# Filter spectra summed in PSUM, and adaLN products placed beside other projections

## The chip, the cores and the metric

One core of one Trainium2 chip runs the whole program. The number that counts is the device time of one execution in microseconds, as the median of several runs.

## The reference, cut to what matters

Two layers run over 1024 latent tokens and 256 context tokens. In each, a mixer (attention, a long convolution called Hyena, and an mLSTM) is followed by a SwiGLU network. Each layer scales and shifts its inputs by 48 groups of 128 numbers made from a conditioning vector (adaLN); the latent tokens use one vector, the context tokens another.

```python
s_lat = jax.nn.silu(c)
s_ctx = jax.nn.silu(c_ctx)
for l in range(DEPTH):
    mod = (s_lat @ w_mod[l] + b_mod[l])[:, None, :]
    mod_c = s_ctx @ w_mod[l] + b_mod[l]
    sh1, sc1, g1, sh2, sc2, g2 = jnp.split(mod, 6, axis=-1)
    ...
    h = modulate(x, norm1_w[l], sh1, sc1)
    hc = modulate(ctx, norm1_w[l], sh1c, sc1c)
    y, yc = token_mixer(h, hc, ...)
    x = x + g1 * y
    x = x + g2 * swiglu(modulate(x, norm2_w[l], sh2, sc2), ...)
```

Inside the mixer the Hyena part needs the spectrum of a filter that a small network makes, for both orders `o`, over the latent length and, in layer 0 only, over the context length:

```python
filt = (z @ w3) * jnp.exp(-t * jnp.abs(decay))
circ = jnp.concatenate([fwd, zeros, jnp.flip(bwd[:L - 1], axis=0)], axis=0)
filt_fft = jnp.fft.rfft(circ, axis=0)
```

## The kernel before, in words

Everything stays in fp32. Most matrix products are made as three products of split halves (a high and a low part), the three lines L168, L169 and L170 in `mm3`; the kernel calls the splits `w` (weights), `hh` and `hl` (tokens). The instructions are written in Python generators; `weave` interleaves several of them by their counts (the second number of each stream, a third number being a head start), a scheduler then fixes one order for each engine, and each engine works through its own order. All weights come by DMAs that SP (SyncE) issues in its order; a tile pool with `bufs` buffers makes a load wait until the buffer's last reader is done, and what stands behind it on SP waits too.

The stages of a layer's first half are written in `project`:

- The key projections (`self.first`) are woven with the first filter taps. In layer 0 this follows the start, where `first_mod` makes adaLN groups 0 to 15 for layer 0 with matmuls.
- The **V/Q stage**: value and query projections (`project_v`, `project_q`), woven with the remaining filter taps. `filter_taps` makes two matmuls, ACT exponentials, a DVE product `ex` (L912), and the sums `eo` (L920 on DVE or POOL) that are stored to memory for each of 8 (latent, tag L) or 2 (context, tag C) residues.
- The **hyena stage**: `hyena_inputs` makes nine blocks of 128 output channels (48 products on 512 columns each and, in layer 0, 24 on 256 columns), convolves them on DVE (L459, L460), and transposes them. Woven with it is `filter_spectra`. In layer 0 alone `modulation` for groups 16 to 47 is woven in as well.

`modulation` makes one group `f` at a time for the conditioning vectors `v`: SP loads 512 KB of weights (`mraw`, L250); for layer 0 DVE multiplies them by the broadcast conditioning row `silb` and adds up each row (the `junk` operation, L263) for the latent vector; POOL multiplies in place for the other vector (L254), ACT adds that up (L271), and POOL adds the bias (L272). The pool `mr` has two `mraw` buffers there.

`filter_spectra` reads the stored taps again (`er`). For each parity `par` and order `o` it makes 14 fp32 matmuls with matrices `mf` (or 2 for the short length), each alone in a PSUM bank out of two pairs (`f0`,`f1` and `t`,`o`). ACT copies the first of a pair to `fsb` (L967), and DVE adds or subtracts the second (one line, L948, for this and for the butterflies that follow, whose names show which is which: those with `fsb` are the sums of the pairs).

In layer 0's second half, the down projection (`down`, weights `raw<-in_wdn`, loaded at L156, activations `raw<-act` at L1415) is woven with `next_mod`, which makes all of layer 1's adaLN groups with POOL and ACT alone: 48 groups for the latent vector and 16 for the context vector, three `mraw` buffers; and with layer 1's `filter_mlp` (its first matmul is L868).

## Time and profile before

| | us |
|---|---|
| median of 3 runs | 3497.43 |
| lowest and highest of them | 3488.84, 3499.35 |
| the profiled execution's own time | 3502.94 |
| span in that profile, first to last instruction | 3501.2 |
| TensorE (PE) busy | 3245.5, 93% |
| VectorE (DVE) busy | 2143.6, 61% |
| ScalarE (ACT) busy | 1383.2, 40% |
| GpSimd (POOL) busy | 1298.2, 37% |

The busy times are over the whole program; a stage can be limited by another engine than the program is. The profiled execution took 1.7 us more than its span.

### The profile page before, as it was taken

To read this page: it belongs to the slowest core of one execution; us is meant where nothing else is said; L and a number is where in the kernel's file an instruction comes from. 1 tells how busy PE (TensorE), PEld (TensorE's weight loads), DVE (VectorE), ACT (ScalarE), POOL (GpSimd) and SP (SyncE) were. 2 spreads that over 40 slices of the span, in tenths; PEclk is the share of its full clock that TensorE was granted. 3 is DMA by queue.
4 is the path that set the end of the run, shared out by engine and by line. 5 is a ranking of instruction groups with operands and counts; after the bars stand their busy time and mean duration, and the time that the engine had idled before them with its cause. 6 is when DMAs were issued, how large, how long until landed. Compare 5 with 4: busy or idle time off the path is not lost. (4 is left out here: it accounts for less than half of the span.)

```text
span 3501.2 us, 49138 instructions
## 1 busy us (share of the span) xinstructions
PE 3245.5 (93%) x17486; PEld 2764.1 (79%) x17486; DVE 2143.6 (61%) x3893; ACT 1383.2 (40%) x3049; POOL 1298.2 (37%) x1192
## 2 busy tenths in 40 slices
PE   7988999888979999998989999999888899999998
PEld 3966798878868888886867897898777578887787
DVE  8669657897494444344565756556995854444443
ACT  5444456433453322223441543355343533333210
POOL 2345323574143333334880220133662443443000
PEclk8999999898989999998999999999899999999999
DMA  6666546432711222126662364445325322223532
GB/s 232 198 198 204 164 129 185 127 92 70 209 61 52 73 72 67 63 68 237 224 223 85 119 207 152 142 122 177 98 78 162 98 73 75 82 76 100 163 97 72
DMA packets 336932, 448.75 MB, mean 128 GB/s; under 512 B 46576, under 2 KB 248996, under 8 KB 334639
## 3 DMA queue, kind: packets, MB, share of 16 engines
q1 hardware_dynamic: 336312, 445.27, 40.2%
q8 instruction: 138, 2.26, 0.3%
q14 instruction: 107, 0.88, 0.1%
q10 hardware_dynamic: 375, 0.34, 0.0%
HBM read 329.34 MB, written 116.16 MB: 127 GB/s over the span
## 5 line engine op out<-in xcount | busy, mean ns | idle before, releaser
L136 ACT ACTIVATE w<-raw 128x512 fp32r<-128x512 f32 (+3 forms) x286 | 221.0, 800 | 479.6 <-PE f L169 133.3
L168 PE MATMUL f<-b,w 128*128 128x512 f32 (+1 forms) x912 | 342.5, 386 | 44.8 <-ACT b L136 37.4
L141 DVE TENSOR_TENSOR w<-raw,w 128x512 fp32r<-128x512 f32 (+3 forms) x266 | 278.6, 1063 | 151.6 <-ACT w L136 139.6
L141 DVE TENSOR_TENSOR w<-S,w 128x512 fp32r<-128x512 f32 x168 | 145.7, 888 | 353.8 <-ACT w L136 332.9
L169 PE MATMUL f<-b,w 128*128 128x512 f32 (+1 forms) x912 | 338.6, 372 | 2.6 <-DVE b L141 2.4
L170 PE MATMUL f<-b,w 128*128 128x512 f32 (+1 forms) x912 | 336.9, 370 | 0.0
L168 PE MATMUL mm<-w,hh 128*128 128x256 f32 (+2 forms) x928 | 280.1, 302 | 9.7 <-ACT hh L326 5.1
L254 POOL TENSOR_TENSOR mraw<-mraw,silb 128x1024 f32<-128x1024 f32 x96 | 248.3, 2593 | 106.1 <-DVE mod L263 67.7
L170 PE MATMUL mm<-w,hl 128*128 128x256 f32 (+2 forms) x928 | 276.6, 300 | 5.3 <-DVE hl L327 5.3
L169 PE MATMUL mm<-w,hh 128*128 128x256 f32 (+2 forms) x928 | 278.6, 301 | 0.0
L1427 DVE SCALAR_TENSOR_TENSOR x<-f,mod,x 128x512 f32<-128x512 f32 (+1 forms) x256 | 166.6, 663 | 168.7 <-PE f L170 159.9
L168 PEld LDWEIGHTS f<-b,w 128*128 128x128 f32 x912 | 179.4, 199 | 84.4 <-ACT b L136 41.8
L169 PEld LDWEIGHTS f<-b,w 128*128 128x128 f32 x912 | 177.2, 194 | 35.9 <-DVE b L141 5.1
L170 PEld LDWEIGHTS f<-b,w 128*128 128x128 f32 x912 | 176.8, 194 | 30.0
L136 ACT ACTIVATE w<-S 128x512 fp32r<-128x512 f32 x168 | 101.1, 626 | 227.2 <-POOL S L1232 208.3
L168 PEld LDWEIGHTS mm<-w,hh 128*128 128x128 f32 x928 | 178.2, 192 | 14.4 <-ACT hh L326 7.1
L170 PEld LDWEIGHTS mm<-w,hl 128*128 128x128 f32 x928 | 176.9, 191 | 7.3 <-DVE hl L327 6.8
L169 PEld LDWEIGHTS mm<-w,hh 128*128 128x128 f32 x928 | 178.1, 192 | 0.8 <-DVE w L141 0.3
L271 ACT ACTIVATE mraw<-mraw 128x1024 f32<-128x1024 f32 x96 | 101.6, 1058 | 147.6 <-POOL mraw L254 147.3
L1294 PE MATMUL a<-hb,w 128*128 128x512 f32 x352 | 141.4, 402 | 7.9 <-DVE hb L141 7.8
L1294 PE MATMUL b<-hb,w 128*128 128x512 f32 x352 | 140.7, 400 | 8.1 <-DVE hb L141 7.9
L168 PE MATMUL mm<-hh,w 128*128 128x512 f32 (+1 forms) x360 | 143.8, 399 | 1.6 <-ACT hu L453 1.6
(685 smaller groups left out, 9255.5 us busy)
## 6 DMA issues: line engine op xcount, KB each, us to landing
mraw<-in_wmodT SPq DMA_DIRECT2D x96, 512.0 KB
raw<-in_wgu SPq DMA_DIRECT2D x88, 512.0 KB
act<-g SPq DMA_DIRECT2D x88, 256.0 KB
raw<-in_wdn SPq DMA_DIRECT2D x44, 512.0 KB
raw<-act SPq DMA_DIRECT2D x42, 512.0 KB
raw<-in_wout SPq DMA_DIRECT2D x32, 512.0 KB
q<-qd SPq DMA_DIRECT2D x144, 96.0 KB
eoL<-eo SPq DMA_DIRECT2D x64, 192.0 KB
```

The lines of the kernel that those rows point to most:

```text
L136: ins = nc.scalar.activation(out=hi, in_=src, func=AF.Copy)
L141: (eng or nc.vector).tensor_tensor(out=lo, in0=src, in1=hi.bitcast(F32), op=ALU.subtract)
L168: nc.tensor.matmul(out=ps, lhsT=ah, rhs=bh, start=(i == 0), stop=False, skip_group_check=on)
L169: nc.tensor.matmul(out=ps, lhsT=ah, rhs=bl, start=False, stop=False, skip_group_check=on)
L170: nc.tensor.matmul(out=ps, lhsT=al, rhs=bh, start=False, stop=(i % part == part - 1 or i == n - 1), skip_group_check=on)
L254: nc.gpsimd.tensor_tensor(out=raw, in0=raw, in1=sil[v], op=ALU.mult)
L271: self.nc.scalar.activation(out=raw, in_=raw, func=AF.Copy, accum_out=o)
L1294: nc.tensor.matmul(out=ps, lhsT=ah[:, ks], rhs=bl, start=False, stop=False, skip_group_check=not start)
L1427: nc.vector.scalar_tensor_tensor(out=x, in0=ps[:, :n], scalar=d["mod"][:, 40 + m, v:v + 1], in1=x, op0=ALU.mult, op1=ALU.add)
```

## The change

**Spectra.** The sum or difference of each pair is now made by two matmuls that add up in one PSUM bank, the second with `mf` or, for a difference, with its negative `mg` (new, loaded in pool "fb" at the start of the hyena stage). That is 16 matmuls for each `par` and `o` in place of 14 (4 in place of 2 for the short length). Of the eight sums five are copied by ACT (before, seven copies), the others are read from PSUM by DVE. Eight DVE sums fall away for each `par` and `o` (two for the short length). The `er` loads get four buffers.

**adaLN.** `silu_row` no longer loads the plain vector and applies Silu: the start stores the Silu rows to memory (`silr`, two DMAs on ACT's queue, each with 1024 separate 4-byte pieces) and the rows are read from there. In both layers `modulation` of groups 16 to 47 is created ahead of the filter taps' pool; the first ME = 12 groups are woven into the V/Q stage and the other 20 into the hyena stage. For layer 1 (latent vector alone, thus POOL and ACT without DVE) these 32 groups are taken out of layer 0's down stage, where 32 of 64 items remain.

```diff
@@ constants
+ME = 12, 12
@@ silu_row
         t = self.t(sp, [P, DM], F32, "silb")
-        self.nc.sync.dma_start(out=t, in_=self.A["crow"][v].partition_broadcast(P))
-        self.nc.scalar.activation(out=t, in_=t, func=AF.Silu)
+        self.nc.sync.dma_start(out=t, in_=self.silr[v].partition_broadcast(P))
         return t
@@ dft_mats
-            M[n] = self.t(hp, [P, R // 2 if n[0] == "n" else R, 2, P], F32, "m" + n)
+            M[n] = self.t(hp, [P, R // 2 if n[0] in "ng" else R, 2, P], F32, "m" + n)
@@ filter_spectra
-        pairs = [(0, 4), (2, 6), (1, 7), (3, 5)] if R == 8 else [(0, 1)]
-        turn = False
+        half = R // 2
+        neg = M["g" + tag]
+        mats = M["f" + tag]
+
+        sums = [("p0", 0, half, 0, 1), ("m0", 0, half, 0, -1)]
+        if R == 8:
+            sums = [("y1", 1, 7, 1, -1), ("x1", 1, 7, 0, 1), ("y3", 3, 5, 1, -1), ("x3", 3, 5, 0, 1)] + sums + [("y2", 2, 6, 1, -1), ("x2", 2, 6, 0, 1)]
+        banks = itertools.cycle(x for y in SB for x in y)
...
-                for pair in pairs:
-                    eo = {}
-                    for r in pair:
-                        eo[r] = new("er", 3)
-                        nc.sync.dma_start(out=eo[r], in_=EO[par][o][:, r, :])
-                    ra, rb = pair
-                    for tri in range(2):
-
-                        comp = par if tri == 0 else 1 - par
-                        if tri == 1 and ra == 0:
-                            continue
-                        turn = not turn
-                        pa, pb = (self.ps(x) for x in SB[turn])
-                        for r, pp in ((ra, pa), (rb, pb)):
-                            nc.tensor.matmul(out=pp[:, :HY], lhsT=mats[:, r, comp, :], rhs=eo[r], start=True, stop=True)
-                        sb = new("fsb", 2)
-                        nc.scalar.activation(out=sb, in_=pa[:, :HY], func=AF.Copy)
-                        if tri == 0:
-                            acc["p", ra] = tt(new(f"accp{ra}"), sb, pb[:, :HY], ALU.add, nc.vector)
-                            if ra == 0:
-                                acc["m", ra] = tt(new("accm"), sb, pb[:, :HY], ALU.subtract, nc.vector)
-                        else:
-                            acc["y", ra] = tt(new(f"accy{ra}"), sb, pb[:, :HY], ALU.subtract, nc.vector)
-                    yield
+                acc, eo = {}, {}
+                for name, ra, rb, tri, sign in sums:
+                    if ra not in eo:
+                        for r in (ra, rb):
+                            eo[r] = new("er", 4)
+                            nc.sync.dma_start(out=eo[r], in_=EO[par][o][:, r, :])
+                    comp = 1 - par if tri else par
+                    ps = self.ps(next(banks))[:, :HY]
+                    mb = mats[:, rb, comp, :] if sign > 0 else neg[:, rb - half, comp, :]
+                    nc.tensor.matmul(out=ps, lhsT=mats[:, ra, comp, :], rhs=eo[ra], start=True, stop=False)
+                    nc.tensor.matmul(out=ps, lhsT=mb, rhs=eo[rb], start=False, stop=True)
+                    if name in ("x3", "y3", "x2"):
+                        acc[name] = ps
+                    else:
+                        acc[name] = new(name)
+                        nc.scalar.activation(out=acc[name], in_=ps, func=AF.Copy)
+                    if name == "y3":
+                        s13 = tt(new("s13"), acc["y1"], ps, ALU.add)
+                        R2 = tt(acc["y1"], acc["y1"], ps, ALU.subtract)
+                    elif name == "x3":
+                        P0 = tt(new("P0"), acc["x1"], ps, ALU.add)
+                        D_ = tt(acc["x1"], acc["x1"], ps, ALU.subtract)
+                    if sign < 0:
+                        yield
...
@@ first_mod
         nc.scalar.activation(out=sil, in_=sil, func=AF.Silu)
+        self.silr = self.dram([2, DM], "silr")
+        for v in range(2):
+            nc.scalar.dma_start(out=self.silr[v].rearrange("(k p) -> p k", p=P), in_=sil[:, :, v])
@@ project
+            sp, silp, mr = (mst.enter_context(self.pool(x, bufs=b, side="right")) for x, b in (("md", 1), ("sl", 2), ("mr", 2)))
+            sil = [self.silu_row(silp, v) for v in range(2 - last)]
+            junk = (DM, lambda: self.t(sp, [P, DM], BF16, "junk"))
+            mods = self.modulation(l, [(f, range(2 - last)) for f in range(16, 48)], mr, "mraw", junk, sil, range(16, 48))
             with self.pool("fa", side="right") as fa:
                 taps = chain(*(self.filter_taps(l, R, t, fa) for t, R in tags))
                 weave((self.first, (10, 4)[l]), (self.take(taps, TK[l]), TK[l]))
                 self.lnexp(False)
                 D["G"] = self.gates(l, D)
-                weave((chain(self.project_v(l, D, pj), self.project_q(l, D, pj)), 10 + nt), (taps, TV[l]))
-            mods = []
-            if l == 0:
...
-                self.lnexp()
...
+                weave((chain(self.project_v(l, D, pj), self.project_q(l, D, pj)), 10 + nt), (taps, TV[l]), (self.take(mods, ME[l]), ME[l]))
             with self.pool("fb") as fb, self.pool("hi", side="right") as hi:
-                weave((self.hyena_inputs(l, D, hi), 18 if last else 27), *((g, 32) for g in mods),
-                      (chain(*(self.filter_spectra(l, R, t, M["f" + t], fb) for t, R in tags)), 36))
-            if l == 0:
-                self.mod_done(0, 4)
+                self.dft_mats(fb, ["g" + t for t, _ in tags], M)
+                weave((self.hyena_inputs(l, D, hi), 18 if last else 27), (mods, 32 - ME[l]),
+                      (chain(*(self.filter_spectra(l, R, t, M, fb) for t, R in tags)), 20 if last else 24))
+            if last:
+                nc.vector.memset(self.L[1]["mod"][:, 16:48, 1], 0.0)
+            self.mod_done(l, 4)
@@ second
-                    m = chain(*(self.next_mod(v, n, sp, mr) for v, n in ((0, 48), (1, 16))))
-                    weave((f, 28), (m, 70, 14), (self.filter_mlp(l + 1, fs), *FW))
-                nc.vector.memset(self.L[1]["mod"][:, 16:48, 1], 0.0)
+                    m = chain(*(self.next_mod(v, n, sp, mr) for v, n in ((0, 16), (1, 16))))
+                    weave((f, 28), (m, 34, 6), (self.filter_mlp(l + 1, fs), *FW))
                 self.mod_done(1, 1)
-                self.mod_done(1, 4)
@@ tables
-        A["mn" + tag] = np.ascontiguousarray(-mf[:, R // 2:].astype(f))
+        A["mg" + tag] = A["mn" + tag] = np.ascontiguousarray(-mf[:, R // 2:].astype(f))
```

The order of instructions, at three places. Numbers at the end of a name count the tiles.

SP in layer 0's down stage, where the loads of adaLN weights (`mraw`) meet those of the down projection (`raw<-in_wdn`, and `raw<-act`). Before:

```order
L250 DMA mraw_17131<-in_wmodT 128x1024
L250 DMA mraw_17157<-in_wmodT 128x1024
L250 DMA mraw_17218<-in_wmodT 128x1024
L156 DMA raw_16461<-in_wdn 128x1024
L250 DMA mraw_17223<-in_wmodT 128x1024
L156 DMA raw_16467<-in_wdn 128x1024
L250 DMA mraw_17296<-in_wmodT 128x1024
L250 DMA mraw_17301<-in_wmodT 128x1024
L156 DMA raw_16473<-in_wdn 128x1024
L250 DMA mraw_17306<-in_wmodT 128x1024
L156 DMA raw_16479<-in_wdn 128x1024
L250 DMA mraw_17367<-in_wmodT 128x1024
```

And now, at the same activations and the same first weights of the down projection:

```order
L252 DMA mraw_17448<-in_wmodT 128x1024
L252 DMA mraw_17453<-in_wmodT 128x1024
L252 DMA mraw_17458<-in_wmodT 128x1024
L1414 DMA raw_16268<-act_2047_9396 128x2x512
L252 DMA mraw_17463<-in_wmodT 128x1024
L1414 DMA raw_16274<-act_2048_9397 128x2x512
L158 DMA raw_16336<-in_wdn 128x1024
L158 DMA raw_16342<-in_wdn 128x1024
L158 DMA raw_16348<-in_wdn 128x1024
L158 DMA raw_16354<-in_wdn 128x1024
```

Before, eight loads of adaLN weights stood ahead of this group's first down weight and more between the weights; now the last loads of adaLN weights of the stage stand ahead of this group's two activations, and its four down weights follow each other.

DVE at the end of layer 0's V/Q stage (`ex` and `eo` are the last filter taps, `w` are weight splits, `junk` with `mod` is one adaLN group). Before:

```order
L912 TENSOR_TENSOR ex_1885<-f_385_1887,ex_1885 128x384
L912 TENSOR_TENSOR ex_1885<-f_386_1891,ex_1885 128x384
L912 TENSOR_TENSOR ex_1885<-f_387_1896,ex_1885 128x384
L912 TENSOR_TENSOR ex_1885<-f_388_1900,ex_1885 128x384
L920 TENSOR_TENSOR eo_1904<-ex_1885 128x768
L141 TENSOR_TENSOR w_2549<-raw_2546,w_2548 128x1024
L141 TENSOR_TENSOR w_2773<-raw_2770,w_2772 128x1024
L263 ISA junk_2085,mod_312<-mraw_2083,silb_2054,bmod_306 128x1024
L263 ISA mod_312 128x1
L263 ISA junk_2154,mod_312<-mraw_2152,silb_2054,bmod_306 128x1024
```

And now:

```order
L265 ISA junk_2740,mod_315<-mraw_2738,silb_638,bmod_309 128x1024
L265 ISA mod_315 128x1
L913 TENSOR_TENSOR ex_1971<-f_412_1977,ex_1971 128x384
L143 TENSOR_TENSOR w_2529<-raw_2526,w_2528 128x1024
L265 ISA junk_2803,mod_315<-mraw_2801,silb_638,bmod_309 128x1024
L265 ISA mod_315 128x1
L143 TENSOR_TENSOR w_2696<-raw_2693,w_2695 128x1024
L913 TENSOR_TENSOR ex_1971<-f_413_1982,ex_1971 128x384
L913 TENSOR_TENSOR ex_1971<-f_414_1986,ex_1971 128x384
L921 TENSOR_TENSOR eo_1990<-ex_1971 128x768
L265 ISA junk_2911,mod_315<-mraw_2909,silb_638,bmod_309 128x1024
```

Before, the first of the adaLN groups came behind the last `eo`; now twenty-one of the 32 stand ahead of it on DVE (the last two of them are in these rows), and two more ahead of the first hyena convolution.

PE in layer 0's hyena stage, within the 512-column products of a block (`mm`). Before, with single matmuls of the spectra (L965):

```order
L168 MATMUL mm_559_2620<-hh_345,w_2548 128x512
L965 MATMUL o_2474<-er_2471,mfL_622 128x384
L169 MATMUL mm_559_2620<-hl_353,w_2548 128x512
L170 MATMUL mm_559_2620<-hh_345,w_2549 128x512
L168 MATMUL mm_559_2620<-hh_346,w_2548 128x512
L169 MATMUL mm_559_2620<-hl_354,w_2548 128x512
L965 MATMUL f_523_2481<-er_2469,mfL_622 128x384
L170 MATMUL mm_559_2620<-hh_346,w_2549 128x512
L466 MATMUL s_2540<-ident,hc_2536 128x128 x2
```

And now, with pairs in one bank (L964 and then L965):

```order
L170 MATMUL mm_492_2356<-hh_351,w_2348 128x512
L964 MATMUL f_456_2203<-er_2199,mfL_625 128x384
L964 MATMUL f_461_2241<-er_2199,mfL_625 128x384
L965 MATMUL f_456_2203<-er_2201,mgL_2151 128x384
L965 MATMUL f_461_2241<-er_2201,mfL_625 128x384
L964 MATMUL t_2250<-er_2246,mfL_625 128x384
L965 MATMUL t_2250<-er_2248,mgL_2151 128x384
L964 MATMUL o_2289<-er_2246,mfL_625 128x384
L965 MATMUL o_2289<-er_2248,mfL_625 128x384
L171 MATMUL mm_492_2356<-hl_359,w_2348 128x512
```

Before, each spectra matmul wrote a bank of its own; now the names show two matmuls for each bank, the differences with `mgL`. PE's last pair of tap matmuls has moved too: 69 products on 256 columns and 20 on 512 columns, behind it in the order before, stand ahead of it now.

## Rows read from the trace of the kernel before

**Rows 1.** Cores: span and mean granted TensorE clock.

```profile
core 0: 3501.2 us, clock 0.956
```

**Rows 2.** Windows: stretch, length, PE, PEld, DVE, ACT, POOL busy, PEclk, DMA share, GB/s.

```profile
97.00:184.60 87.60, 87.15 (x682) 85.53 (x681) 49.93 (x87) 40.20 (x73) 32.33 (x37) 1.00 0.62 196
184.60:402.90 218.30, 190.86 (x860) 144.61 (x859) 183.11 (x220) 100.97 (x179) 107.09 (x86) 0.96 0.61 196
1760.00:1860.00 100.00, 89.73 (x399) 71.87 (x399) 73.97 (x73) 46.73 (x71) 72.99 (x51) 0.93 0.64 211
1950.00:2095.00 145.00, 142.85 (x1077) 138.04 (x1077) 99.69 (x204) 83.31 (x180) 46.11 (x65) 1.00 0.53 175
2095.00:2239.50 144.50, 144.50 (x613) 109.91 (x611) 83.70 (x130) 50.52 (x82) 2.27 (x23) 1.00 0.47 147
```

**Rows 3.** Waits of PE in layer 0's hyena stage: us in total, times, longest.

```profile
PE f L965 <- DVE accm L948: 6.8, 2, 4.7
```

**Rows 4.** Lines by form, DVE, same stage: busy, mean ns | idle before.

```profile
L263 DVE CUSTOM_DVE_ANT_0 junk<-mraw,silb,bmod 128x1024 bf16<-128x1024 f32 x32 | 42.8, 1337 | 15.2 <-DMA mraw<-in_wmodT 15.0
...
L948 DVE TENSOR_TENSOR P<-accp,accp 128x384 f32<-128x384 f32 x4 | 7.4, 1848 | 0.1
...
L948 DVE TENSOR_TENSOR accp<-fsb,f 128x384 f32<-128x384 f32 x10 | 5.5, 546 | 2.5 <-DMA FC<-accp 2.4
```

**Rows 5.** Lines by form, POOL, same stage.

```profile
L254 POOL TENSOR_TENSOR mraw<-mraw,silb 128x1024 f32<-128x1024 f32 x32 | 87.6, 2738 | 67.8 <-DVE mod L263 67.7
```

**Rows 6.** Lines by form, DVE, in layer 1's hyena stage.

```profile
L948 DVE TENSOR_TENSOR P<-accp,accp 128x384 f32<-128x384 f32 x4 | 2.2, 558 | 0.1
```

**Rows 7.** Timeline of PE, products on 256 columns: start us, length us.

```profile
182.03 0.28 PE L169 MATMUL mm<-w,hh 128*128 128x256 f32 x1
...
183.83 0.28 PE L169 MATMUL mm<-w,hh 128*128 128x256 f32 x1
```

**Rows 8.** Timeline of PE, 512-column products and spectra matmuls.

```profile
2108.83 0.40 PE L170 MATMUL mm<-hh,w 128*128 128x512 f32 x1
...
2110.24 0.39 PE L170 MATMUL mm<-hh,w 128*128 128x512 f32 x1
...
2113.46 0.81 PE L965 MATMUL o<-er,mfL 128*128 128x384 f32 x2
2114.10 0.81 PE L965 MATMUL f<-er,mfL 128*128 128x384 f32 x2
```

**Rows 9.** Timeline of SP's queue, in layer 0.

```profile
90.84 0.53 SPq L389 DMA_DIRECT2D dkT<-et  x1
...
180.78 1.20 SPq L277 DMA_DIRECT2D silb<-in_crow  x2
...
196.23 0.33 SPq L250 DMA_DIRECT2D mraw<-in_wmodT  x1
...
205.03 0.33 SPq L250 DMA_DIRECT2D mraw<-in_wmodT  x1
```

**Rows 10.** Timeline of DVE, the end of layer 0's V/Q stage and behind it.

```profile
175.93 0.56 DVE L912 TENSOR_TENSOR ex<-f,ex 128x384 f32<-128x384 f32 x1 [0.31 <-PE f L911]
...
190.15 1.28 DVE L263 CUSTOM_DVE_ANT_0 junk<-mraw,silb,bmod 128x1024 bf16<-128x1024 f32 x1
```

**Rows 11.** Tile `mraw` up to 500 us: min/median/max ns, first and last start.

```profile
L263 DVE CUSTOM_DVE_ANT_0 junk<-mraw,silb,bmod x32: 1268/1277/2252, 190.2 to 376.2; 128x1024 bf16<-128x1024 f32 x32
```

**Rows 12.** Timeline of SP's queue and of PE, layer 0's down stage.

```profile
1734.21 21.52 SPq L250 DMA_DIRECT2D mraw<-in_wmodT  x8
...
1757.61 0.33 SPq L156 DMA_DIRECT2D raw<-in_wdn  x1
...
1758.03 2.07 PE L868 MATMUL f<-ft,w 66*128 66x512 f32 x2 [9.40 <-DVE x L1427]
```

**Rows 13.** A window of the start, and a DMA queue over 0 to 60 us.

```profile
5.00:40.00 35.00, 35.00 (x80) 7.73 (x80) 27.65 (x56) 11.63 (x22) 0.80 (x1) 1.00 1.00 381
...
q10 hardware_dynamic: 375, 0.34, 2.0%
```

More of the change, by code (lines that the diff above doesn't have):

```diff
@@ L1 @@
+import itertools
 from contextlib import ExitStack
@@ new lines, in tt @@
+                def tt(out, a, b, op):
+                    nc.vector.tensor_tensor(out=out, in0=a, in1=b, op=op)
+                    return out
+                acc, eo = {}, {}
[22 more added lines that the diff above has]
+                        yield
@@ L979, in filter_spectra @@
                 if R == 2:
[L980 to L981 removed]
+                    put(0, acc["p0"])
+                    put(1, acc["m0"])
                     continue
                 stt = nc.vector.scalar_tensor_tensor
[L984 to L990 removed]
+                E_ = tt(new("E"), acc["p0"], acc["x2"], ALU.add)
+                P2 = tt(acc["p0"], acc["p0"], acc["x2"], ALU.subtract)
+                put(4, tt(new("fo", 2), E_, P0, ALU.subtract))
                 put(0, tt(P0, E_, P0, ALU.add))
                 P3 = E_
[L993 to L998 removed]
+                stt(out=P3, in0=D_, scalar=-RH, in1=acc["m0"], op0=ALU.mult, op1=ALU.add)
+                P1 = acc["m0"]
+                stt(out=P1, in0=D_, scalar=RH, in1=P1, op0=ALU.mult, op1=ALU.add)
+                y26 = acc["y2"]
+                R1, R3 = D_, y26
                 stt(out=R1, in0=s13, scalar=RH, in1=y26, op0=ALU.mult, op1=ALU.add)
@@ L1545, in project @@
         last = l == DEPTH - 1
-        tags = self.tags(l)
+        nc, tags = self.nc, self.tags(l)
         nt = 8 if last else 10
@@ L1558, in project @@
                 D["G"] = self.gates(l, D)
-                weave((chain(self.project_v(l, D, pj), self.project_q(l, D, pj)), 10 + nt), (taps, TV[l]))
-            mods = []
-            if l == 0:
-                sp = mst.enter_context(self.pool("md", side="right"))
-                silp = mst.enter_context(self.pool("sl", bufs=2, side="right"))
-                mr = mst.enter_context(self.pool("mr", bufs=2, side="right"))
-                sil = [self.silu_row(silp, v) for v in range(2)]
-                self.lnexp()
-                junk = (DM, lambda: self.t(sp, [P, DM], BF16, "junk"))
-                mods = [self.modulation(0, [(f, (0, 1)) for f in range(16, 48)], mr, "mraw", junk, sil, range(16, 48))]
-            with self.pool("fb") as fb, self.pool("hi", side="right") as hi:
-                weave((self.hyena_inputs(l, D, hi), 18 if last else 27), *((g, 32) for g in mods),
-                      (chain(*(self.filter_spectra(l, R, t, M["f" + t], fb) for t, R in tags)), 36))
-            if l == 0:
-                self.mod_done(0, 4)
+                weave((chain(self.project_v(l, D, pj), self.project_q(l, D, pj)), 10 + nt), (taps, TV[l]), (self.take(mods, ME[l]), ME[l]))
+            with self.pool("fb") as fb, self.pool("hi", side="right") as hi:
+                self.dft_mats(fb, ["g" + t for t, _ in tags], M)
[4 more added lines that the diff above has]
+            self.mod_done(l, 4)
     def mix_heads(self, l, D, mix, hg):
@@ L1849, in _layout @@
     A["ccol"] = np.stack([c[0], c_ctx], axis=1).reshape(KB, P, 2).transpose(1, 0, 2)
-    A["crow"] = np.stack([c[0], c_ctx], axis=0)
     A["bmod"] = b_mod.reshape(L, 48, P).transpose(0, 2, 1)
```

21 lines of the change are left out of this document (1 added, 20 removed).

## The prediction

> **What bounds the kernel now.** I began with the view of cores: one core, 3501.2 us, granted clock 0.956 [rows 1]. TensorE is busy for 93% of that, so the first question is in which stretches it is not, and the view of windows answers it for the stages that the change touches [rows 2]. Three are full or nearly so: layer 0's V/Q stage (PE 87.15 of 87.60 us), layer 1's V/Q stage (142.85 of 145.00) and layer 1's hyena stage (144.50 of 144.50). Two are not. In layer 0's hyena stage PE is busy for 190.86 of 218.30 us, while DVE is busy for 183.11; what PE waits for there is DVE's spectra sums [rows 3]. In layer 0's down stage PE is busy for 89.73 of 100 us in the stretch shown and its clock is 0.93; DMA share is 0.64.
>
> How much of the 218.3 us could go? Layer 1's hyena stage does the same latent work with PE full, in 144.5 us. Layer 0 adds the context: 9 blocks of 24 products on 256 columns at 0.12 us (15 steps in 1.80 us [rows 7]) are 25.9 us, 8 spectra matmuls at 0.64 us (the step between the two in [rows 8]) are 5.1, and 18 transposes, which I price like the nearest small product, 2.2. That floor is 177.7 us, so some 41 us are lost now, partly idle and partly to a clock of 0.96. The same stage holds all 32 adaLN groups: 42.8 us of DVE [rows 4] and 87.6 of POOL [rows 5].
>
> **The change, part by part.**
>
> *Spectra, PE.* Each of four (parity, order) rounds gets two more matmuls for the long length and, in layer 0, two more for the short one: 16 in layer 0, 8 in layer 1, at 0.64 us [rows 8]: +10.2 and +5.1 us. PE is full in layer 1, so that is paid there in full. The `mg` loads (half of `mf`) come at the start of a stage with DMA share 0.61 or less and are costed at nothing: the hyena products cover them. If the first difference had to wait, the bank alone waits, a few us.
>
> *Spectra, DVE.* 40 sums of about 0.546 us [rows 4] fall away in layer 0 (21.8 us) and 32 in layer 1 (17.5). In layer 1 DVE has 60 us to spare, so nothing comes of it.
>
> *Hyena stage, layer 0.* 23 of 32 `junk` operations move ahead of the first hyena convolution: 23 x 1.34 = 30.8 us of DVE. Left are 183.1 - 21.8 - 30.8 = 130.5 us of DVE against 177.7 + 10.2 = 188 us of PE. DVE no longer limits the stage, and the whole 41 us can come back: best case -41 + 10.2 = -31 us.
>
> *V/Q stage, layer 0: what the moved groups cost.* This is the term I trust least. On DVE the last taps now stand behind the 21st `junk`, and PE's last pair of tap matmuls waits in turn for what DVE frees. Before, the last `ex` was at 175.93 [rows 10]. PE has 69 x 0.12 + 20 x 0.235 (six steps in 1.41 us [rows 8]) = 13.0 us more work ahead of its last pair, so it starts to wait if the taps end later than about 188.9. When does the 21st group come? The loads now stand right behind the last key store, issued at 90.84 and over at 91.37, and the first `junk` came 9.4 us after the `silb` issue [rows 9, 10]: about 100.7. Then one group every p us. The nearest rows bound p. Two buffers turned over in 8.80 us when nothing else pressed (the two `mraw` issues with one between them [rows 9]): 4.4 us a group. Over the hyena stage with a crowded DVE it was (376.2 - 190.2) / 31 = 6.0 us [rows 11]. The V/Q stage has less on DVE (49.93 of 87.60 us) than the hyena stage, but SP there also issues tap stores in order; I take the middle, 5.2. Then the 21st is at 100.7 + 20 x 5.2 = 204.7, a wait of 16 us. At 4.4 it is none, at 6.0 it is 32. Behind DVE's late taps are queued its weight splits for the first hyena block, which is why I add 5 us for what the remaining groups and this backlog still cost (0 to 10). Layer 0 up to the mixer: -41 + 10.2 + 16 + 5 = **-10 us**.
>
> *Contention.* A POOL product lengthens DVE operations beside it: the butterfly sum `P` takes 1848 ns in layer 0, where POOL runs the products [rows 4], and 558 ns in layer 1, where POOL is idle [rows 2, 6]. The sum with one operand in PSUM takes 546 ns in the very stage where the other takes 1848 [rows 4]. The mean hold is 1.3 us, well under a POOL product of 2738 ns. The Trainium skill, "SBUF — State Buffer", section "Who interferes with whom", says that DVE's second port pair is shared with GpSimd under an exclusive lock, so that a DVE instruction with two SBUF inputs and a GpSimd one cannot run together. These rows agree in kind; by the mean hold the sum is the one here, by a full hold for each product it is the slower rival's below.
>
> *Down stage, layer 0.* Half of the 64 items go. SP now spends 21.52 us on eight adaLN loads in a row ahead of the next down weight, and PE then idles 9.40 us [rows 12]; 10.3 us more are idle in the 100 us after it [rows 2], and the clock of 0.93 costs some 7 in those. Now the loads end ahead of that point and the weights follow each other. Bounds 0 (other waits take over: DVE is busy for 74 of the 100) and -25; I take **-15**.
>
> *Layer 1.* The 32 groups use POOL (32 x 2.74 = 88 us) and ACT in stages of 145 us where POOL is busy for 46 and 2 us [rows 2]; they fit. With 5.1 us of matmuls and 1 for contention: **+6** (5 to 15, the upper end if DVE's 99.7 of 145 us in the V/Q stage grows by a hold for each of its 12 products, 33 us).
>
> *Start.* The Silu rows leave by two ACT-queue DMAs with 2048 pieces of 4 bytes. The stretch 5 to 40 us has DMA share 1.00, with PE waiting on weights at the DMAs' pace, so their time counts. The nearest small packets are those of queue q10, 375 in 2.0% of 16 engines over 60 us, 51 ns each [rows 13]: 2048 x 51 / 16 = 6.5 us. Bounds 0 and 6.5, I take **+3**. The Trainium skill, "DMA: Bandwidth & Descriptors", section "Rules for kernel authors", wants transfers coalesced into large ones; no row of before shows such a DMA, so whether it is paid here is open.
>
> *Sum.* -10 - 15 + 6 + 3 = -16 us: the profiled execution's 3502.9 would be 3487. That execution is 5.5 us above the median of the runs, 3497.4, so on the median I forecast 3481 (-0.5%), and write 3480.
>
> **The rivals.** A measurement of this kernel can tell about 0.3% (10.5 us) from no change.
>
> *Much better.* p is 4.4, no backlog, the whole down loss returns: -31 - 25 + 5 + 0 = -51, 3446 us. For it: the two-buffer turn of 8.80 us. Against it: only few groups kept that pace.
>
> *The wait moves into V/Q (no change).* p is 6.0 as in the hyena stage: layer 0 is -41 + 10.2 + 32 + 5 = +6, the sum 0, 3497 us. For it: that is the mean over 31 groups. Against it: DVE is less crowded here.
>
> *Down gains nothing (no change).* Of the adaLN loads four still stand in a row on SP ahead of the group's activations; if PE's wait forms there, the sum is -16 + 14 = -2, 3495 us. Against it: none stands between the down weights.
>
> *Slower.* Every POOL product holds DVE for its whole length in the V/Q stages. Then a group costs DVE 1.34 + 2.74 plus its share of what else is there, 49.93 / 21 = 2.4: p = 6.5. The 21st is at 230.7, a wait of 42 us; layer 0 is +16, layer 1 +15, the sum -15 + 16 + 15 + 3 = +19, 3516 us. It decides from p = 6.0, where the sum is zero, and shows as slower from about 6.5. Against it: the mean hold of 1.3 us [rows 4, 6].
>
> **How the numbers follow.** Forecast 0.50 (its own range 3470 to 3487); much better 0.14; wait moves into V/Q 0.12; down gains nothing 0.08; slower 0.16. Faster by over 0.3%: 0.50 + 0.14 = 0.64; within 0.3%: 0.20; slower: 0.16. The range runs from 3452 to 3505: it leaves out most of the slower case and the extreme of the better one, under 0.2 together.
>
> **What would show it.** In the profile of the changed kernel: the spacing of `junk` rows in the V/Q stage (4.4, 5.2 or 6 and more), PE's longest wait near the last `ex`, PE full in layer 0's hyena stage at about 188 us; layer 1's hyena stage near 150 us with PE full; the 9.40 us wait and the 21.52 us of SP's loads gone from the down stage; the first key projection later by the `silr` stores' time. I would be wrong if the V/Q stage of layer 0 grew by over 30 us, if the down stage kept its length, or if the 4-byte pieces cost far more than 51 ns each: these pieces have no near row, and at ten times that price they alone would turn the sign.

## The result

The changed kernel takes 3537.74 us against 3493.14 before: ratio 1.0121, 95% interval 1.0100 to 1.0143, so it is slower by 1.2%. I had forecast 3480. The span of the profiled execution grew by 34.5 us, from 3501.2 [rows 1] to 3535.7 us.

To see where, I cut both timelines at the same four instructions: the first key product of each layer and the last product of each hyena stage (on 256 columns in layer 0, on 512 in layer 1). The table's segments are differences of those starts; the later runs stand in it too, each from its one profiled execution. The segment between a layer's two cuts is called its stretch below.

| kernel | first key product | layer 0 to end of hyena | to layer 1's first key product | layer 1 to end of hyena | rest | end |
|---|---|---|---|---|---|---|
| before, us | 56.3 | 346.3 | 1561.9 | 274.8 | 1261.9 | 3501.2 |
| changed, minus before | +10.8 | +7.0 | -23.0 | +29.6 | +10.1 | +34.5 |
| forecast | +3 | -10 | -15 | +6 | 0 | -16 |
| e1_mods_only | +12.3 | +3.5 | -21.0 | +25.5 | -2.0 | +18.3 |
| e1_spectra_only | -0.8 | +2.4 | +4.1 | +5.2 | +14.8 | +25.7 |
| e1_layer1_back | +11.2 | +8.8 | -3.3 | +5.5 | +11.3 | +33.5 |
| e1_late_rows | +10.8 | +4.7 | -22.5 | +28.9 | +7.7 | +29.6 |
| e2_row_store | +0.7 | +5.6 | -19.7 | +29.3 | +7.8 | +23.7 |
| e2_spectra_early | +12.8 | +9.7 | -20.1 | +35.7 | +3.7 | +41.8 |
| e2_l1_no_loads | +11.8 | +7.2 | -23.1 | +14.3 | +5.0 | +15.2 |
| e2_l1_no_product | +11.6 | +9.2 | -25.9 | +14.3 | +1.5 | +10.7 |
| e3_l1_buffers | +12.0 | +10.6 | -22.4 | +22.3 | +11.6 | +34.1 |
| e3_l1_hyena_only | +13.4 | +6.6 | -25.7 | +28.9 | +4.7 | +27.9 |
| e3_spectra_only_early | +0.6 | +4.2 | +1.2 | +7.1 | -9.2 | +3.9 |
| e3_half_l1 | +0.4 | +0.7 | -16.2 | +12.9 | +2.7 | +0.5 |
| e4_l1_no_sum | +12.6 | +8.3 | -20.6 | +34.5 | +7.1 | +41.9 |
| e4_l1_sum_only | +12.5 | +5.2 | -19.4 | +9.4 | +9.7 | +17.4 |
| e4_up | 0.0 | +0.4 | -5.7 | +1.4 | -5.6 | -9.5 |
| e5_l0_no_product | +1.0 | -15.8 | -24.5 | +32.4 | +7.1 | +0.2 |
| e5_up_pairs | -0.4 | +0.1 | -1.6 | +6.7 | -8.8 | -4.0 |

Segments that are the same in several kernels show the noise. Layer 0's stretch lies between +4.7 and +10.6 in the nine kernels that have both the changed start and the changed layer 0, layer 1's between +28.9 and +32.4 in the five that have it as the changed kernel does, and the last segment, 1262 us long, is 5.6 us shorter in e4_up without an edit in it. So a step of 5 us in one execution is at the edge of what can be read.

Now the stages, in windows with the columns of [rows 2], between the same instructions in both kernels: layer 0 from the V/Q stage on and its hyena stage, then layer 1 from its first key product and its hyena stage. Before:

```profile
87.00:184.60 97.60, 97.15 (x759) 95.53 (x758) 56.32 (x98) 45.40 (x83) 35.02 (x43) 1.00 0.61 196
184.60:402.60 218.00, 190.56 (x857) 144.31 (x856) 182.81 (x220) 100.97 (x179) 107.09 (x86) 0.96 0.61 196
1964.50:2095.40 130.90, 128.75 (x976) 124.40 (x975) 88.74 (x181) 74.42 (x159) 43.70 (x63) 1.00 0.53 176
2095.40:2239.30 143.90, 143.90 (x610) 109.49 (x609) 83.30 (x130) 50.09 (x81) 2.27 (x23) 1.00 0.48 148
```

The changed kernel:

```profile
97.80:219.40 121.60, 102.18 (x729) 97.65 (x728) 98.68 (x129) 65.32 (x122) 96.39 (x75) 0.94 0.71 230
219.40:420.40 201.00, 191.24 (x895) 149.12 (x895) 110.55 (x149) 76.54 (x133) 42.27 (x56) 0.98 0.52 170
1959.30:2105.60 146.30, 132.30 (x972) 125.02 (x971) 98.00 (x180) 88.58 (x188) 84.65 (x90) 0.98 0.66 215
2105.60:2263.70 158.10, 151.47 (x625) 113.61 (x624) 75.42 (x85) 64.06 (x108) 49.33 (x62) 0.98 0.56 182
```

PE was nearly full in layer 1 before (2.2 us idle); now it is idle for 14.0 us of the first of its windows and 6.6 us of the hyena stage, and its clock is 0.98. In layer 0 the hyena stage is shorter (201.0 for 218.0 us), but 19.4 us of idle time stand in the V/Q window, which had 0.45 us of it. DVE there is busy for 98.68 of 121.60 us. Over layer 0's whole stretch PE's idle time is what it was (35.5 us before, 35.6 now), although DVE is busy for 238 us of it in place of 269.

**The start.** SP's queue in the changed kernel, what SP waited for (waits, 6 to 40 us), and queue q10 over 0 to 60 us:

```profile
6.21 1.01 SPq L158 DMA_DIRECT2D raw<-in_w_mk  x2
21.86 0.81 SPq L1519 DMA_DIRECT2D mraw<-in_wm  x2
30.18 7.03 SPq L1486 DMA_DIRECT2D x<-in_xin  x8
...
SPq L1519 <- DMA silr<-sil: 14.6, 1, 14.6
SPq L1486 <- DMA silr<-sil: 7.5, 1, 7.5
...
q10 hardware_dynamic: 2455, 0.35, 4.1%
```

The third pair of weight loads comes at 21.86 us; in the trace of before it was issued at 7.05. The two stores of 4-byte pieces take much longer than their packets' time, and SP stands still behind them.

**The down stage.** PE's longest wait there before was 9.40 us [rows 12]. Now (waits of PE, 1700 to 1960 us):

```profile
PE f L170 <- DVE x L1426: 5.3, 2, 4.4
PE f L170 <- ACT b L138: 3.7, 1, 3.7
```

**The pace in layer 0's V/Q stage.** `junk`, the first and the 21st of 32:

```profile
109.58 1.29 DVE L265 CUSTOM_DVE_ANT_0 junk<-mraw,silb,bmod 128x1024 bf16<-128x1024 f32 x1 [4.26 <-DMA mraw<-in_wmodT]
...
225.10 1.27 DVE L265 CUSTOM_DVE_ANT_0 junk<-mraw,silb,bmod 128x1024 bf16<-128x1024 f32 x1
```

(225.10 - 109.58) / 20 = 5.8 us a group. PE's waits there are many and short; the largest sum of them (waits of PE, 67 to 219.4 us) is

```profile
PE f L911 <- DVE ex L913: 8.6, 6, 2.4
```

### The profile page after: what moved, and what is told of

It is laid out like the page before. It is cut to its first block, busy times and chain, and to the rows that moved or that the text cites. A ratio compares the mean times of both kernels' runs of the same rounds, so it can differ in the third digit from the quotient of the medians.

```text
span 3535.7 us, 49084 instructions
## 1 busy us (share of the span) xinstructions
PE 3259.7 (92%) x17534; PEld 2774.2 (78%) x17534; DVE 2086.5 (59%) x3821; ACT 1368.1 (39%) x3031; POOL 1284.0 (36%) x1192
## 5 line engine op out<-in xcount | busy, mean ns | idle before, releaser
L143 DVE TENSOR_TENSOR w<-raw,w 128x512 fp32r<-128x512 f32 (+3 forms) x266 | 287.8, 1097 | 191.0 <-ACT w L138 183.9
L256 POOL TENSOR_TENSOR mraw<-mraw,silb 128x1024 f32<-128x1024 f32 x96 | 240.4, 2509 | 109.0 <-DMA mraw<-in_wmodT 65.9
```

Source lines behind the costliest of these rows:

```text
L143: (eng or nc.vector).tensor_tensor(out=lo, in0=src, in1=hi.bitcast(F32), op=ALU.subtract)
L256: nc.gpsimd.tensor_tensor(out=raw, in0=raw, in1=sil[v], op=ALU.mult)
```

## The experiments

**First four: the change in halves.** e1_mods_only keeps the new adaLN places and takes back `filter_spectra`; e1_spectra_only is the reverse.

```diff
 # e1_mods_only, against the changed kernel
-(chain(*(self.filter_spectra(l, R, t, M, fb) for t, R in tags)), 20 if last else 24)
+(chain(*(self.filter_spectra(l, R, t, M["f" + t], fb) for t, R in tags)), 36)   # before's function
 # e1_layer1_back
-m = chain(*(self.next_mod(v, n, sp, mr) for v, n in ((0, 16), (1, 16))))
+m = chain(*(self.next_mod(v, n, sp, mr) for v, n in ((0, 48), (1, 16))))   # and no mods in layer 1
 # e1_late_rows: the three silr lines moved to the end of first_mod
```

> The new places of the adaLN products with the spectra of before (single matmuls, DVE sums). Theory A (the loss of layer 1, some 41 us between its first key projection and the end of its hyena stage, comes from the adaLN products put beside its full stages): layer 1 still loses 30 to 40 us, the start 11, the down stage still gains some 22; about 3525 us. Theory B (it comes from the new spectra: 8 more matmuls and their later end): layer 1 loses under 10 us and the time is about 3500.

> The new spectra alone, all adaLN products where they were before. Theory A: layer 1 is 5 us longer (8 matmuls at 0.64 us), layer 0's hyena stage keeps its 218 us within 10, so the time is 3490 to 3505. Theory B: layer 1 alone loses 25 us or more and the time is over 3515.

> The changed kernel with layer 1's 32 adaLN groups put back into layer 0's down stage; layer 0's early groups, the stored Silu rows and the new spectra stay. Theory A: layer 1 gets back all but 5 us of its 41, the down stage loses its 22 again: about 3538 - 36 + 22 = 3524. Theory B: layer 1 keeps 25 us or more of its loss, so the time stays at 3540 or more.

> The changed kernel, but the two stores of the Silu rows in 4-byte pieces are issued behind the last of the first adaLN matmuls (about 45 us) instead of at 4 us. If these pieces hold up the weight loads of the start, the first key projection comes back from 67.1 to about 57 us and the time falls by some 10 us to 3528. If the start is late for another reason (the order of the loads), it stays at 67 and the time at 3538.

The 41 us that layer 1 loses in these expectations are the table's +29.6 and +10.1 together, of which the second lies behind the hyena stage. Measured: 3521.97 (ratio 1.0065, 1.0040 to 1.0090), 3527.51 (1.0081, 1.0058 to 1.0104), 3544.18 (1.0134, 1.0108 to 1.0159) and 3536.33 us (1.0110, 1.0087 to 1.0133). Neither theory holds alone: both halves lose. The groups make the stretch of layer 1 25.5 us longer and nothing behind it; the spectra make it 5.2 longer and lose 14.8 us behind it. With layer 1's groups back in the down stage the stretch is +5.5, as theory A says, but the down stage takes its 20 us back and the 11 us behind the hyena stage stay, so the time does not fall (3524 was expected). e1_late_rows tested nothing: the scheduler issued the stores at 4.1 us again, since only `sil` holds them.

**The start.**

```diff
 # e2_row_store
-for v in range(2):
-    nc.scalar.dma_start(out=self.silr[v].rearrange("(k p) -> p k", p=P), in_=sil[:, :, v])
+srow = self.t(mr, [2, DM], F32, "srow", 1)
+nc.scalar.dma_start(out=srow, in_=A["crow"])
+nc.scalar.activation(out=srow, in_=srow, func=AF.Silu)
+nc.scalar.dma_start(out=self.silr, in_=srow)
```

> The changed kernel, but the Silu rows are made from the plain vectors on two partitions and stored by one DMA in two pieces of 4096 bytes in place of 2048 pieces of 4. In the changed kernel SP waited 14.6 and 7.5 us for the silr stores at the start. If that is the 11 us by which the start is late, the first key projection comes at 56 to 58 us (67.1 there, 56.3 before) and the time falls by about 10 us. If the pieces only take the place of another wait, it stays above 63 us.

3526.54 us (1.0085, 1.0069 to 1.0102), and the first key product is back, as the timeline shows of it and then of the changed kernel:

```profile
56.98 0.59 PE L170 MATMUL mm<-w,hh 128*128 128x272 f32 x1 [4.83 <-ACT hh L327]
```

```profile
67.14 0.59 PE L170 MATMUL mm<-w,hh 128*128 128x272 f32 x1 [4.83 <-ACT hh L327]
```

**The end of the spectra.** The number in the weave is the count over which a stream is spread: 16 steps over 36 end early, over 20 late.

```diff
 # e2_spectra_early, and the same in e3_spectra_only_early
-(chain(*(self.filter_spectra(l, R, t, M, fb) for t, R in tags)), 20 if last else 24)
+(chain(*(self.filter_spectra(l, R, t, M, fb) for t, R in tags)), 36)
```

> The changed kernel with the count of the spectra stream in the weave set to 36 as before, in place of 24 and 20, so that the spectra end earlier in the hyena stage. Theory C (what the spectra lost in layer 1 is their later end, 2251 to 2265 us against 2211, behind which the next stage's loads stand): the last spectra matmul of layer 1 comes 25 us or more before the last 512-column product, and the step of 12 us that layer 1 loses behind its hyena stage goes; time 10 to 15 us lower. Rival: the loss comes from the matmuls themselves or from DVE, and the time stays within 5 us.

> The new spectra alone (adaLN as before), with the weave count 36 as before. Theory C (the later end of the spectra costs 10 to 15 us behind layer 1's hyena stage, since the next stage's loads and pools stand behind them): the spectra end about 2215 us, layer 1 loses 6 to 10 us in place of 20, the time is 3503 to 3512 in place of 3527. Rival: layer 1 loses 15 us or more still.

3533.91 us (1.0120, 1.0101 to 1.0138), and 3508.89 us (1.0045, 1.0030 to 1.0060) for the spectra alone, 18.6 us less than with the late end. The last spectra matmul of layer 1 comes at 2203.7 us (2251.4 in e1_spectra_only). The 40 us behind the last 512-column product, in e1_spectra_only and then in e3_spectra_only_early (windows):

```profile
2250.20:2270.20 20.00, 16.78 (x101) 16.02 (x100) 11.78 (x23) 6.17 (x12) 3.82 (x5) 0.91 0.52 151
2270.20:2290.20 20.00, 16.51 (x103) 15.81 (x102) 9.02 (x29) 9.63 (x29) 8.81 (x12) 0.91 0.64 207
```

```profile
2252.40:2272.40 20.00, 20.00 (x140) 19.96 (x139) 8.75 (x18) 9.88 (x23) 3.33 (x5) 1.00 0.60 172
2272.40:2292.40 20.00, 20.00 (x146) 19.96 (x146) 13.48 (x39) 9.28 (x29) 11.72 (x15) 1.00 0.38 121
```

6.7 us idle and a clock of 0.91 in the other 33 (3 us) are some 10 us. PE waits there twice, for ACT to copy the attention's first products out of PSUM (timeline of PE, ACT and SP, e1_spectra_only; last, SP in e3_spectra_only_early):

```profile
2263.01 0.41 PE L169 MATMUL mm<-w,hh 128*128 128x320 f32 x1 [3.22 <-ACT va L487]
2275.63 0.41 PE L169 MATMUL mm<-w,hh 128*128 128x320 f32 x1 [3.33 <-ACT va L487]
...
2259.38 1.09 ACT L469 ACTIVATE hst<-s 128x512 f32<-128x512 f32 x2 [6.84 <-PE s L467]
2262.73 0.23 ACT L487 ACTIVATE va<-mm 128x64 f32<-128x64 f32 x1 [0.57 <-DMA FL<-y]
2273.62 1.06 ACT L137 ACTIVATE w<-raw 128x1024 fp32r<-128x1024 f32 x1 [8.32 <-DMA raw<-in_w_mo]
...
2267.15 0.85 SPq L157 DMA_DIRECT2D raw<-in_w_mo  x2
```

```profile
2242.04 0.34 SPq L157 DMA_DIRECT2D raw<-in_w_mo  x1
```

Before the first wait ACT has stood idle for 6.84 us with the copy of the transposes, which comes ahead of `va` in its order here and behind it with the early spectra; a spectra store that has to leave adds 0.57 us. Before the second ACT waits 8.32 us for a weight load. SP issues the first of these loads at 2267.15, 17 us behind the last 512-column product, and with the early spectra 10 us ahead of it. So theory C holds for the spectra alone, and 10 of the 18.6 us are located. Over the table the last segment is +1.5 to +14.8 us in the twelve kernels with the late end and -9.2 to +3.7 in the six others. With layer 1's groups in the same stage (e2_spectra_early) the step behind it falls from +10.1 to +3.7, but the stretch grows by 6 in its one profiled execution, and the ratio stays where it was: the time within 5 us that its expectation gave to the rival.

**What a group costs in layer 1.** Seven kernels, all from the changed one except the last.

```diff
 # e2_l1_no_loads: no load in layer 1's stages, in0=sil[v]    # e2_l1_no_product: no POOL product there
-            nc.sync.dma_start(out=raw, in_=self.A["wmodT"][l, f])
+            if l == 0 or skew:
+                nc.sync.dma_start(out=raw, in_=self.A["wmodT"][l, f])
 # e4_l1_sum_only: both. e4_l1_no_sum: 8 columns in ACT's sum
 # e3_l1_buffers
-(("md", 1), ("sl", 2), ("mr", 2))
+(("md", 1), ("sl", 2), ("mr", 2 + last))
 # e3_l1_hyena_only
-ME = 12, 12
+ME = 12, 0
 # e3_half_l1, against the kernel before: groups 32 to 47 woven into layer 1's hyena stage
-((0, 48), (1, 16))
+((0, 32), (1, 16))
```

> The changed kernel without the 32 loads of adaLN weights in layer 1's V/Q and hyena stages: POOL multiplies the conditioning row by itself, so these 32 groups are left out of the computation while POOL, ACT and their holds on DVE stay. Theory D (layer 1's stages lose to SP and the DMAs: loads that wait for a buffer hold up the stores and loads behind them): layer 1 gets back 20 us or more between its first key projection and the end of its hyena stage. Theory E (they lose to POOL's hold on DVE's operations): it gets back under 7 us.

> The changed kernel with layer 1's 32 loads but without POOL's products on them in the V/Q and hyena stages (ACT adds up the plain weights; the products are left out of the computation). Theory D: layer 1 gets back under 10 us, since the loads and their places on SP stay. Theory E: it gets back 15 us or more.

> The changed kernel with three buffers for layer 1's adaLN weights in place of two. In the changed kernel SP stood still 33.3 us in layer 1's stages, waiting for ACT to finish with a buffer. Theory F (SP's standing is what delays the tap stores and weight loads behind it): with a third buffer SP waits under 15 us there and layer 1 gets back 10 us or more. Theory G (DVE held by POOL's products while they meet with the loads): SP's waits fall but layer 1 gets back under 5 us.

> The changed kernel with none of layer 1's 32 groups in its V/Q stage, all in its hyena stage. If the 15 us by which that V/Q stage is longer come from its 12 groups, it is again within 4 us of before (145 us from the first key projection's landmark), and the hyena stage grows by what 12 more groups cost there: under 8 us if the 3 us a group of POOL time has room (32 x 2.7 = 88 of 150), so the time falls by 7 to 12 us. If the groups cost the same wherever they stand, the time stays within 4 us.

> The kernel before, in which only groups 32 to 47 of layer 1 are moved from layer 0's down stage into layer 1's hyena stage (spectra, Silu rows and layer 0 as before). The down stage should give 8 to 15 of the 22 us that the whole move gave there, and layer 1's hyena stage, where POOL is busy for 2 us, lose 3 to 8: 3485 to 3493. If the groups cost what they cost in the changed kernel, some 0.8 us each, it is even: 3490 to 3500.

> The changed kernel in which ACT adds up 8 of the 1024 columns of layer 1's 32 products (the rest of each sum is left out), with loads and POOL products as they are. From the first key product of layer 1 to its last 512-column product the changed kernel takes 304 us, without loads or without products 289, with the new spectra alone 280. Theory H (the 9 us that stay without loads or without products are ACT's row sums, 40 us of ACT work between the copies that free PSUM): the stretch takes 293 to 297 us. Theory I (loads and products cost 9 us each by themselves and the rest together): it stays at 301 to 305.

> The changed kernel with ACT's 32 row sums in layer 1 taken over the conditioning row, without the loads of weights and without POOL's products, which are left out. Theory H: the stretch still takes 286 to 290 us. Theory I: it falls to 280 to 283, as with the new spectra alone.

Medians, in this order: 3521.18, 3515.83, 3532.64, 3540.56, 3506.32, 3541.54 and 3520.40 us. The stretch from the first key product to the last 512-column product takes 280.0 us with the new spectra alone, 284.2 with ACT's sums alone, 289.1 with sums and products, 289.1 with sums and loads, 304.4 with all three, and 309.3 with the sums cut to 8 columns. So the sums are not what is dear: cutting them brings nothing back, and theory H falls (theory I's own figures are missed by 1 and 4 us). Loads or products added to the sums alone cost 4.9 us each, hardly more than the noise, but both together cost 20.2: more than twice their sum. Taking the products away brings back 15.3 us, as theory E has it; taking the loads away brings back as much, which neither D nor E allowed. The two are not quite even, for in e2_l1_no_loads POOL multiplies the resident row by itself, and these products are shorter. DVE's weight splits show the meeting (lines by form): before, the changed kernel, without loads, without products.

```profile
L141 DVE TENSOR_TENSOR w<-raw,w 128x1024 fp32r<-128x1024 f32 x13 | 15.9, 1222 | 24.1 <-ACT w L136 24.1
```

```profile
L143 DVE TENSOR_TENSOR w<-raw,w 128x1024 fp32r<-128x1024 f32 x13 | 24.3, 1866 | 42.3 <-ACT w L138 37.3 <-DMA dkT<-et 4.4 <-PE mm L171 0.5
```

```profile
L143 DVE TENSOR_TENSOR w<-raw,w 128x1024 fp32r<-128x1024 f32 x13 | 19.1, 1484 | 35.2 <-ACT w L138 35.2
```

```profile
L143 DVE TENSOR_TENSOR w<-raw,w 128x1024 fp32r<-128x1024 f32 x13 | 15.9, 1220 | 48.7 <-ACT w L138 27.9 <-DMA er<-eoL 15.0 <-PE f L913 5.8
```

How PE comes to wait is in the rows. In layer 1's stretch its longest waits are not for a split but for DVE's tap product `ex` and convolution `hc` (timeline of the changed kernel, PE, DVE and POOL, at the two longest):

```profile
2033.86 0.69 PE L911 MATMUL f<-w3h,zr 128*128 128x384 f32 x1 [4.75 <-DVE ex L913]
2030.06 3.28 DVE L143 TENSOR_TENSOR w<-raw,w 128x1024 fp32r<-128x1024 f32 x1 [4.41 <-DMA dkT<-et]
2029.90 2.35 POOL L256 TENSOR_TENSOR mraw<-mraw,silb 128x1024 f32<-128x1024 f32 x1
...
2156.16 1.09 PE L467 MATMUL s<-ident,hc 128*128 128x128 f32 x4 [5.25 <-DVE hc L461]
2147.13 2.35 DVE L243 SCALAR_TENSOR_TENSOR A<-mod,n 128x16 f32<-128x16 f32 x1
2147.05 2.40 POOL L256 TENSOR_TENSOR mraw<-mraw,silb 128x1024 f32<-128x1024 f32 x1
2152.12 2.69 DVE L952 TENSOR_TENSOR P<-E,P 128x384 f32<-128x384 f32 x1
2151.83 2.58 POOL L256 TENSOR_TENSOR mraw<-mraw,silb 128x1024 f32<-128x1024 f32 x1 [0.77 <-DMA mraw<-in_wmodT]
```

Each of the three DVE operations starts just after a POOL product has started and ends only once that has ended. In e2_l1_no_product `A` takes 0.18 us and `P` 0.56. `ex` and `hc` stand behind these operations on DVE, and PE's two waits for them are 10 of the 20.6 us that it is idle in the stretch. In front of the first, DVE had also waited 4.41 us for a DMA.

POOL's product, with loads and without (lines by form):

```profile
L256 POOL TENSOR_TENSOR mraw<-mraw,silb 128x1024 f32<-128x1024 f32 x32 | 78.8, 2467 | 36.0 <-DMA mraw<-in_wmodT 36.0
```

```profile
L257 POOL TENSOR_TENSOR mraw<-silb 128x1024 f32<-128x1024 f32 x32 | 62.4, 1952 | 2.9 <-DMA silb<-silr 2.9
```

The loads do not make that difference. Over single products, one takes 2.40 us at a DMA share of 0.00 and 2.39 at 1.03 in the changed kernel, and 1.89 at 0.00 and at 0.98 in e2_l1_no_loads: what differs is that there both inputs are one tile. With the loads, POOL waits 36.0 us for them, and its products start from 2025.5 to 2177.9 us; without, from 2024.2 to 2126.9. But in either kernel four of the 13 splits take longer beside a product, so why loads and products cost more together stays open. A third buffer took SP's waits for ACT in layer 1 from 33.3 us to 15.4 and the stretch from 304.4 to 297.1, between what the two theories wanted. e3_l1_hyena_only tested nothing: its 32 products start at 2024.5 to 2176.6 us, 16 of them ahead of the hyena stage's first product as in the changed kernel, because the scheduler put them there again. Where the groups stand is answered by e3_half_l1, whose 16 products all start inside the hyena stage: it gains 16.2 and loses 12.9 us (ratio 1.0035, 1.0022 to 1.0048; 3485 to 3500 was expected). That is 0.8 us a group, as for the 32 over both stages in e1_mods_only (25.5 us).

**Another place.**

```diff
 # e4_up, against the kernel before; one buffer in "mru"
-list(self.up(l, B, hc, sp, act, w, ...))
+sil = {0: self.silu_row(su, 0)}
+m = self.modulation(1, [(f, (0,)) for f in range(16, 48)], mu, "mraw", None, sil, range(48))
+weave((up, 200), (m, 32))
```

> The kernel before, with layer 1's groups 16 to 47 moved from layer 0's down stage to its up stage (one buffer, spread over the whole stage), where the page shows TensorE at 9 tenths or more, DMA at 1 to 2 tenths and POOL at 3. If a group costs only where DVE's weight splits and SP's stores stand close behind each other, the up stage loses under 5 us, the down stage gives 15 to 22, and the time is 3475 to 3485. If any group costs 0.8 us beside a full TensorE, it is even: 3490 to 3500. Should SP stand for the one buffer, weights come late and it is slower than 3500.

> The kernel before with layer 1's 32 groups beside layer 0's up stage (e4_up, whose profile was 9 us shorter than that of before and whose median was even), and the new spectra in layer 1 alone with the weave count 36, where they gained some 3 us when alone. If these add up: 3483 to 3493. If the up stage takes all that the down stage gives, it is even within 0.3% of before.

e4_up takes 3496.35 us (1.0011, 0.9998 to 1.0025): no change, as its expectation has it for groups that cost 0.8 us each. Its own up stage is 19 us longer, at 0.6 us a group, and the down stage gives some 25 back. With the new spectra in layer 1 alone (e5_up_pairs) it is 3506.03 us (1.0023, 1.0009 to 1.0036), though its profiled execution is 4 us shorter than that of before: the two gains do not add up, and no version here beats the kernel before.

**Layer 0.**

```diff
 # e5_l0_no_product, against e2_row_store
-nc.gpsimd.tensor_tensor(out=raw, in0=raw, in1=sil[v], op=ALU.mult)
+if l == 1 or skew:
+    nc.gpsimd.tensor_tensor(out=raw, in0=raw, in1=sil[v], op=ALU.mult)
```

> The kernel with the rows stored in two pieces (e2_row_store) without POOL's 32 products in layer 0 (they are left out of the computation; loads, DVE's junk operations and ACT's sums stay). If POOL's hold on DVE makes layer 0's idle time, the stretch from its first key product to its last 512-column product falls from 352 to 325 to 338 us and junk takes 1.27 us in place of 1.56. If the loads and DVE's own work make it, the stretch stays above 345.

3503.02 us (1.0028, 1.0015 to 1.0040). The stretch falls from 351.9 to 330.5 us. The two windows, e2_row_store first:

```profile
57.00:408.90 351.90, 313.78 (x1754) 264.85 (x1755) 237.67 (x315) 161.26 (x288) 159.54 (x146) 0.96 0.57 184
```

```profile
57.30:387.80 330.50, 310.01 (x1753) 262.70 (x1754) 204.38 (x315) 161.13 (x288) 67.77 (x114) 0.97 0.61 196
```

PE's idle time falls from 38.1 to 20.5 us while the loads stay, and DVE's same 315 operations take 33 us less. So the products hold up layer 0. DVE's weight splits take 1391 ns there, and 2012 with the products. But their hold on DVE is not the only thing that goes with them: the groups also come every 4.5 us in place of 6.2, and POOL is busy for 68 us in place of 160. No run separates these. `junk` fell from 1.56 to 1.37 us, not to the 1.27 that was expected.

## Why the prediction was wrong, step by step

**Spectra on PE: right.** 8 matmuls at 0.64 us were to cost layer 1 5.1 us; e1_spectra_only shows 5.2 with PE idle 3 us of 280.

**Spectra, what was left out: +10 us.** I read the diff's weave count as a detail. It moved the last spectra matmul of layer 1 from 2210.6 to 2264.9 us, behind the hyena stage's end, and ACT's copies and a weight load of the next stage came late. The step that failed is a missing term: the sum prices the spectra's matmuls and DVE's sums and puts what stands behind the hyena stage at nothing. It looked at busy time ("DVE has 60 us to spare"), not at what becomes free when.

**Layer 1's groups: mechanism wrong, +24 us where I put 1.** The failed step is "they fit", from POOL's busy time. POOL had the room; DVE's operations that PE's work stands behind did not: the splits took 1222 ns before and 1866 now, and PE waits for `ex` and `hc` behind such operations. I had priced that hold at 1 us, with 15 as the upper bound of layer 1 together. The mean hold of 1.3 us, on which I put the slower rival aside, hides what the rows show: an operation that a product catches waits until the product ends (the splits up to 3.40 us), and the mean is lower because others meet none.

**Layer 0: +7 where I had -10.** The groups came at 5.8 us, not at the 5.2 that I took as the middle; the rival "the wait moves into V/Q" had 6.0 and +6 us for layer 0, and that is what this layer did. The 21st group is at 225.10 us, forecast 204.7: 9 us of that are the late start, 12 the pace. So the V/Q stage grew by 24 us ((219.4 - 67.1) - (184.6 - 56.3)) where I had 16, and the hyena stage gave back 17 net of the new matmuls, where I had 26 (-31 + 5). The one long wait at the last tap matmuls that I forecast did not come: PE's idle time is spread over waits of at most 2.9 us. The second failed step is "DVE no longer limits the stage, and the whole 41 us can come back". It rests on reading [rows 3] as what PE waits for, and that row is 6.8 of 27.4 us of idle time. e1_spectra_only takes these sums away (DVE is busy for 30 us less) and the stretch is no shorter (+2.4), with PE waiting 10.6 us for DVE's convolution `hc`; e1_mods_only moves the groups and its PE is still idle for 42 us of the stretch, in place of 35. DVE's share of busy time did not tell the wait. POOL's products make it (e5_l0_no_product: -21.4 us without them), and they go wherever the groups go; that they do it by their hold on DVE is likely, not shown. The contention paragraph had both rows for this and priced it only in the slower rival. That rival's 6.5 us a group did not come in the changed kernel.

**Down stage: right, undersized.** -23.0 for -15; the wait of 9.40 us is gone.

**Start: right in kind, undersized.** +10.8 for +3 (bounds 0 and 6.5). The price of 51 ns a packet was too high: queue q10's share over 60 us rose from 2.0% to 4.1%, 20 us of packet time over 16 engines for 2080 packets, 10 ns each. The step that failed is that only packet time counts; SP stood 14.6 and 7.5 us for the stores to land, while the DMAs moved 49 to 152 GB/s for some of that time. [rows 13] does not show PE waiting on weights either, for PE is busy in all 35.00 us of it; that the start goes at the loads' pace is shown by e2_row_store.

Together: +8 (start) + 17 (layer 0) - 8 (down) + 24 (layer 1) + 10 (behind it) = +51 us, from -16 to +35. One slip changes little: with nothing from the down stage the rival's sum is -16 + 15 = -1, not -2.

By the Trainium skill, "DMA: Bandwidth & Descriptors", section "Rules for kernel authors", many small transfers are to be coalesced. This case agrees and gives its price: two 4096-byte pieces in place of 2048 of 4 took the start from 67.1 back to 57.0 us. By the Trainium skill, "SBUF — State Buffer", section "Who interferes with whom", a DVE instruction with two SBUF inputs contends with a GpSimd instruction that reads SBUF, over a port pair that is an exclusive lock. The trace agrees: splits take 1866 ns on average beside products and 1220 without, and the held ones end behind the product.

What stays open: why loads and products together cost 20 us and either without the other 5; by which road the products hold up layer 0, and the 20 us of idle time that it keeps without them; and the rest of the 18.6 us that the late end of the spectra costs, beyond the 10 located.

## What to carry to other kernels

An engine's idle share does not say that work placed there is free: ask which operations of the other engines it lengthens, and whether those are the ones that TensorE waits for. Where a stage's helper stream is woven in, look at when its last instruction comes, since the next stage's first loads and copies can stand behind it. A DMA in 4-byte pieces in a stretch that lives on weight loads cost the loads behind it here, not its own bytes. And before a variant is read, look in its trace whether the order really changed: two of these did not.

## What was not expected of the hardware

2048 four-byte writes of 8 KB in all held SP's next loads up for 14.6 and 7.5 us. A DVE operation on 128x16 elements took 2.35 us beside a POOL product, and 0.18 us in the run without products. POOL's product on 128x1024 took 1.89 us when both its inputs were one tile and 2.40 when they were two, at a low and at a high DMA share alike.
